# A two-layer decoder trunk on one core: 256-column score and value products in parts, an alternating token order behind attention groups, rotary tables in steps

## The chip, the cores and the metric

One core of one Trainium2 chip runs the kernel; the metric is the device time in microseconds. Matrix products run on TensorE, elementwise work on VectorE and ScalarE, weights come from memory by DMA queues that SyncE issues. In the views of the profile PE is TensorE, PEld its weight load, DVE is VectorE, ACT is ScalarE, POOL is GpSimd and SP is SyncE.

## The reference

Two layers on 256 tokens, a model width of 2048, 16 heads of 128. Each layer is: RMS norm, mixer, residual; RMS norm, gated feed-forward with a causal convolution of width 3, residual; an embedding projected and gated, residual.

```
layer 0 mixer: q,k,v = h @ w_in
   heads 0..7  : stick-breaking: z = q k^T * scale (strictly causal)
                 w = exp(log_sigmoid(z) + suffix sum of log_sigmoid(-z));  out = w @ v
   heads 8..15 : q,k partly rotated (first 32 of 128), three dilated windows
                 mixed by their log-sum-exp;  out = p @ v
layer 1 mixer: q,k,v and 16 forget gates from one projection
   s = q k^T * scale + c_q - c_k  (c: running sum of log gates), causal softmax;  out = p @ v
both: h += out @ w_out
feed-forward: u = conv3(norm(h) @ w_up);  h += (silu(gate) * value) @ w_down
embedding: h += sigmoid(norm(h) @ w_gate) * (p[i] @ w_ple)
```

## The kernel before

**Products in parts.** The activations lie with features on partitions and tokens along the free axis: `X` and `Y` are tiles of 128 partitions by 16 (or up to 16) feature blocks by 2 parts by 256 tokens. Each float32 number is held as two numbers of the type `F32R`, a high part (a copy that is rounded) and a low part (the difference). A product takes three matmuls, high by high, high by low and low by high: `PARTS = ((0, 0), (0, 1), (1, 0))`, line 206. Weights are read from DRAM in one stream in the order of use and split into parts on the chip: ScalarE casts (line 176), VectorE subtracts (line 177).

**The stream of weight products.** A unit is up to four blocks of 128 rows by 256 columns of a weight matrix. `gemm_unit` (line 208) makes up to 24 matmuls of 256 tokens from a unit, with the weight as the stationary operand; `gemm_v` (line 243) makes the values, with tokens as the stationary operand and 256 weight columns moving; `gemm_vf` (line 256) does so with 272 columns for the first values of layer 1 and the gates. `unit` (line 183) has three units split ahead, in a ring of four.

**Attention between units.** Each finished unit is a tick. `defer(n, fn)` (line 194) puts a function at the n-th tick from now, and `tick` (line 197) runs what is due. `head_pair` (line 579) makes q, k and v of two heads with four units each and defers the attention of the pair among the units that follow: `first` (scores and softmax or stick-breaking, 2 to 4 ticks after k), `second` (4 or 5 ticks later) and `attend` (2 ticks later). So a pair's scores stand behind its values, its second step inside the next pair's q or k, its values product inside the next pair's k. TensorE takes its work in this order; the other engines are ordered by a planner unless a place is marked to keep the program's order. `norm_finish` defers the norm's sums and rows; `with_rows` holds back what needs the rows.

**The attention's matmuls** before the change are in full float32, except the suffix sums of the stick-breaking heads (lines 459 to 467), which are in parts, and the row of the gates' sums (line 481):

- `sb_first`, line 438 (128 columns, keys of the second half) and line 441 (256 columns, keys of the first half by all queries).
- `sm_first`, line 483 (128 columns, first half of the queries) and line 485 (256 columns, second half of the queries by all keys).
- `sm_second`, line 520: six transposes of 128x128 of the softmax's weights, then one copy of 768 columns out of PSUM (line 522).
- `attend`, line 529 (128 columns) and line 532 (256 columns): values by weights.

A float32 matmul shows as two records in the trace, a matmul on parts as one. q and k lie in tiles `q` and `k`, the scaled values in `v` (written at lines 588 and 621 by ScalarE).

**The rotary tables** (`rope_tables`, line 401) are sines and cosines of 32 rows by 256 tokens, some twenty VectorE operations with two ScalarE sines, called after pair 1 of layer 0 and first read by `rope` for pair 4. The page's names for tiles: `psq`, `psk`, `psv`, `pso`, `psu`, `psd`, `psg`, `psp` are the products of the weight matrices (q, k, v, output, up, down, gate, embedding), `scs` the scores, `sps` the second step, `avp` the values product.

Of the kernel before, what the change touches and what calls it, by code (L numbers as in the profile page):

```python
# [104 lines left out]
def trunk(ctx: ExitStack, tc: tile.TileContext, xT, pT, pos, gains, conv, bf, cst, wst, out):  # L105
# [20 lines left out]
    rT = cpool.tile([P, 2], F32, name="rT")  # L126

    root = cpool.tile([P, 2], F32, name="root")
# [19 lines left out]
    at = {"group": 0, "off": 0, "unit": 0, "tick": 0, "rows": 0}  # L148
# [58 lines left out]

    def gemm_unit(ps, act, kind, l, c0, k0, first, last, koff=0):

        kc, w = unit(kind, l, k0, c0)  # L210
        order = [(j, k, n) for j in range(2) for k in range(kc) for n in range(3)]
        if at["tick"] == 0:

            order.sort(key=lambda o: o[2])
        for i, (j, k, n) in enumerate(order):
            s, t = PARTS[n]
            nc.tensor.matmul(ps[:, j, :], lhsT=w[:, k, s, j * P:(j + 1) * P], rhs=act[:, k0 - koff + k, t, :],  # L217
                             start=first and i == 0,
                             stop=last and k == kc - 1 and n == 2, skip_group_check=True)
        tick()  # L220
# [22 lines left out]
    def gemm_v(ps, act, l, c0):  # L243

        for i in range(4):
            kc, w = unit("w_in", l, 4 * i, c0)
            for t in range(2):
                tsl = slice(t * P, (t + 1) * P)
                for k in range(kc):
                    for n, (a, b) in enumerate(PARTS):  # L250
                        nc.tensor.matmul(ps[:, t], lhsT=act[:, 4 * i + k, a, tsl], rhs=w[:, k, b],  # L251
                                         start=i + t + k + n == 0,
                                         stop=i == 3 and k == kc - 1 and n == 2, skip_group_check=True)
            tick()
# [146 lines left out]
    def rope_tables():  # L401
        ang = t2_tile("ang", (32, S))
        n = t2_tile("angn", (32, S))
# [4 lines left out]
        for step in (4096.0, 1.0):  # L408
# [13 lines left out]
        nc.vector.scalar_tensor_tensor(out=n, in0=ang, scalar=-1.0, in1=ang,  # L422
                                       op0=ALU.mult, op1=ALU.min)
        nc.vector.tensor_scalar_add(out=n, in0=n, scalar1=math.pi / 2)
        nc.scalar.activation(out=rc, in_=n, func=AF.Sin)
# [9 lines left out]
    def sb_first(q, k):  # L435
# [4 lines left out]
        for j in range(2):  # L440
            nc.tensor.matmul(sc[:, 0, j * S:(j + 1) * S], lhsT=k[:, j, 0:128], rhs=q[:, j, :],
                             start=j == 0, stop=True, skip_group_check=True)
# [14 lines left out]
    def sb_second(z, e, eh, el):  # L457
# [3 lines left out]
        for i, x in enumerate((eh, el)):  # L461
# [6 lines left out]
                         start=False, stop=True, skip_group_check=True)  # L468
        nc.vector.tensor_sub(out=z, in0=z, in1=sp.rearrange("p a b -> p (a b)")[:, :768])
        nc.scalar.activation(out=e, in_=z, func=AF.Exp)  # L470
        return e
# [3 lines left out]
    def sm_first(q, k, fox):  # L475
        sc = at_tile("scs")
        for j in range(2):
            if fox is not None:
# [6 lines left out]
            nc.tensor.matmul(sc[:, j, 128:384], lhsT=q[:, j, 128:256], rhs=k[:, j, :],  # L485
                             start=False, stop=True, skip_group_check=True)
# [27 lines left out]
    def sm_second(pe, s):  # L514
# [10 lines left out]
    def attend(hp, w, v, dst):  # L525
        av = at_tile("avp")
        for j in range(2):
            js = slice(j * P, (j + 1) * P)
            nc.tensor.matmul(av[:, 0, j * S + 128:(j + 1) * S], lhsT=v[:, 1, js],  # L529
                             rhs=w[:, 512 + j * P:512 + (j + 1) * P], start=j == 0, stop=False,  # L530
                             skip_group_check=True)
            nc.tensor.matmul(av[:, 0, j * S:(j + 1) * S], lhsT=v[:, 0, js], rhs=w[:, j * S:(j + 1) * S],  # L532
                             start=False, stop=True, skip_group_check=True)
# [45 lines left out]
    def head_pair(l, hp, act, dst, st):  # L579
        q = work.tile([P, 2, S], F32, name="q", tag="qkv", bufs=2)  # L580
        k = work.tile([P, 2, S], F32, name="k", tag="qkv", bufs=2)
        v = work.tile([P, 2, S], F32, name="v", tag="v", bufs=1)
        full = _cuts(KT)
        if l % 2 == 1 and hp == 0:
            ps = at_tile("psv")
            gemm_vf(ps, act, l)
            for t in range(2):
                nc.scalar.activation(out=v[:, t, :], in_=ps[:, t, 0:S], func=AF.Copy,
                                     scale=rT[:, t:t + 1])
            st["fox"] = forget_gates(l, ps)  # L590
        ps = mm_tile("psq")
# [7 lines left out]
        def first():  # L599
            if l % 2 == 0 and hp < 4:  # L600
                a = sb_first(q, k)
                defer(5, lambda: second(lambda: sb_second(*a)))
            else:
                a = sm_first(q, k, st["fox"] + (2 * hp,) if l % 2 == 1 else None)
# [9 lines left out]

        defer(late + (2 + (l % 2 == 0 and hp >= 4) if hp == 7 or (l % 2 == 1 and hp == 0) else 4), first)
# [4 lines left out]
        for i in range(2):  # L620
            nc.scalar.activation(out=v[:, i, :], in_=ps[:, i, :], func=AF.Copy, scale=rT[:, i:i + 1])
# [29 lines left out]
    for l in range(DEPTH):  # L651
        st = {}
        if l == 0:
# [13 lines left out]
            norm_finish(True, 12, 14)  # L667
        for hp in range(NH // 2):
# [3 lines left out]
            if l % 2 == 0 and hp == 1:  # L672
                rope_tables()
# [158 lines left out]
```

## Time and profile before

| | |
|---|---|
| time, median of 3 runs | 2422.07 us (2421.6 to 2423.37) |
| profiled execution, time and span | 2423.39 us, 2421.6 us |
| mean granted TensorE clock | 0.998 |
| DMA | 458.05 MB, mean 189 GB/s |
| weight products of w_up (`psu`, line 217) | 8448 matmuls, 959.7 us |
| weight products of w_down (`psd`, line 217) | 4224 matmuls, 479.7 us |
| casts of weights (line 176), ScalarE | 874, 901.2 us |
| differences of weights (line 177), VectorE | 874, 1045.8 us |

The profile is of one execution. Its page gives busy times of each engine, the chain of work that ended last (followed back from the last instruction), and groups of instructions with count, busy time and mean duration. Matmuls are pipelined: a record's duration (some 276 ns) overlaps the next one's, so the time that a matmul costs is read from the distance of the starts, or from the chain's pieces, whose length is the time that they hold the chain.

### The profile page before, as it was taken

The page shows a single profiled execution, that of the slowest core. Times are in us where ns is not written, and L with a number is a line of the kernel's source. Part 1 is how long each engine was busy: PE and PEld are TensorE (multiplying, and loading weights), DVE is VectorE, ACT ScalarE, POOL GpSimd, SP SyncE. Part 2 cuts the span into 40 slices and gives each one's busy share as a digit, 9 for nine tenths or more (in the row PEclk, how much of TensorE's full clock was granted, in tenths as well). Part 3 has the DMA queues.
Part 4 walks back from the last instruction along what each step waited for, and adds up shares of the span by engine and source line. Part 5 has one row for each costly group of instructions (what it writes and reads, how often), then busy time and mean ns, then how long its engine had stood idle before and what let it go on. Part 6 is the DMA issues. An engine that isn't in the chain of part 4 may idle for free.

```text
span 2421.6 us, 47927 instructions
## 1 busy us (share of the span) xinstructions
PE 2406.9 (99%) x20992; PEld 2400.8 (99%) x20992; DVE 1581.7 (65%) x2066; ACT 1228.6 (51%) x1546; POOL 5.9 (0%) x13
## 2 busy tenths in 40 slices
PE   9999999999999999999999999999999999999998
PEld 9999999999999999999999999999999999999997
DVE  7666766776567657767755555667665776567666
ACT  6554455554355445555554444555544554455554
POOL 0000000000000000000000000000000000000000
PEclk9999999999999999999999999999999999999999
DMA  7454445555555555555554454555555555555553
GB/s 284 167 181 171 174 182 192 192 193 193 196 197 197 186 199 192 193 186 203 183 188 174 167 181 163 198 190 195 192 192 193 194 195 191 202 193 187 186 203 122
DMA packets 66818, 458.05 MB, mean 189 GB/s; under 512 B 7552, under 2 KB 7840, under 8 KB 16944
## 3 DMA queue, kind: packets, MB, share of 16 engines
q1 hardware_dynamic: 66576, 454.93, 53.0%
q8 instruction: 164, 2.69, 0.4%
q14 instruction: 46, 0.38, 0.0%
q0 software_dynamic: 32, 0.06, 0.0%
HBM read 452.86 MB, written 2.10 MB: 188 GB/s over the span
## 4 chain that ended last, share of the span: by engine, by line
PE 98%; DMA 1%; DVE 0%; SPq 0%; ACT 0%; issue 0%; POOLq 0%; DVEq 0%; ACTq 0%
PE psu L217 40%; PE psd L217 20%; PE psk L217 7%; PE pso L217 7%; PE psq L217 7%; PE psv L251 7%; PE psg L217 7%; DMA wr<-in_w 1%; PE avp L532 1%; PE psv L264 1%; PE psp L217 0%; PE pse L730 0%; PE scs L485 0%; PE sps L520 0%; PE avp L529 0%; PE scs L483 0%
## 5 line engine op out<-in xcount | busy, mean ns | idle before, releaser
L177 DVE TENSOR_TENSOR w<-wr,w 128x1024 fp32r<-128x1024 f32 (+2 forms) x874 | 1045.8, 1198 | 686.0 <-ACT w L176 681.4
L176 ACT CAST w<-wr 128x1024 fp32r<-128x1024 f32 (+2 forms) x874 | 901.2, 1031 | 1063.1 <-PE psu L217 354.3
L217 PE MATMUL psu<-act,w 128*128 128x256 f32 x8448 | 959.7, 276 | 0.0
L217 PEld LDWEIGHTS psu<-act,w 128*128 128x128 f32 x8448 | 958.4, 188 | 0.1
L217 PE MATMUL psd<-act,w 128*128 128x256 f32 x4224 | 479.7, 276 | 0.0
L217 PEld LDWEIGHTS psd<-act,w 128*128 128x128 f32 x4224 | 479.2, 188 | 0.0
L217 PE MATMUL psk<-act,w 128*128 128x256 f32 x1536 | 184.8, 279 | 0.0
L217 PE MATMUL psq<-act,w 128*128 128x256 f32 x1536 | 183.1, 279 | 1.1 <-DVE act L285 0.9
L217 PEld LDWEIGHTS psk<-act,w 128*128 128x128 f32 x1536 | 180.0, 188 | 0.8
L217 PEld LDWEIGHTS psq<-act,w 128*128 128x128 f32 x1536 | 178.7, 188 | 2.1 <-DVE act L285 1.1
L217 PE MATMUL pso<-act,w 128*128 128x256 f32 x1536 | 176.5, 277 | 0.0
L217 PEld LDWEIGHTS pso<-act,w 128*128 128x128 f32 x1536 | 175.6, 188 | 0.1
L251 PE MATMUL psv<-w,act 128*128 128x256 f32 x1440 | 167.4, 277 | 0.0
L251 PEld LDWEIGHTS psv<-w,act 128*128 128x128 f32 x1440 | 165.6, 188 | 0.1
L217 PE MATMUL psg<-act,w 128*128 128x256 f32 x1440 | 164.8, 276 | 0.0
L217 PEld LDWEIGHTS psg<-act,w 128*128 128x128 f32 x1440 | 163.9, 188 | 0.1
L630 DVE TENSOR_TENSOR u<-psu,rb 128x512 f32<-128x512 f32 x88 | 60.9, 692 | 33.0 <-PE psu L217 32.8
L636 DVE SCALAR_TENSOR_TENSOR yv<-u,cv,yv 128x256 f32<-128x256 f32 x176 | 73.4, 480 | 0.0
L636 DVE SCALAR_TENSOR_TENSOR yg<-u,cv,yg 128x256 f32<-128x256 f32 x176 | 73.3, 479 | 0.0
L633 ACT ACTIVATE yg<-u,cv 128x256 f32<-128x256 f32 x88 | 48.0, 593 | 1.1 <-DVE u L630 1.1
L633 ACT ACTIVATE yv<-u,cv 128x256 f32<-128x256 f32 x88 | 47.9, 592 | 0.0
L275 ACT CAST act<-yg 128x512 fp32r<-128x512 f32 x44 | 27.4, 622 | 39.2 <-DVE yg L646 39.2
(165 smaller groups left out, 880.7 us busy)
## 6 DMA issues: line engine op xcount, KB each, us to landing
wr<-in_w SPq DMA_DIRECT2D x388, 1024.0 KB, 4.8
wr<-in_w SPq DMA_DIRECT2D x36, 768.0 KB, 4.3
wr<-in_w SPq DMA_DIRECT2D x8, 896.0 KB, 4.6
h<-in_x SPq DMA_DIRECT2D x4, 512.0 KB, 9.0
wr<-in_w SPq DMA_DIRECT2D x4, 512.0 KB, 10.5
out_dram<-h SPq DMA_DIRECT2D x7, 256.0 KB, 2.4
wr<-in_w SPq DMA_DIRECT2D x2, 816.0 KB, 4.3
pl<-in_w SPq DMA_DIRECT2D x3, 512.0 KB, 7.9
```

What stands on the lines that cost most here:

```text
L176: nc.scalar.copy(out=w[:, :, 0, :], in_=raw)
L177: nc.vector.tensor_sub(out=w[:, :, 1, :], in0=raw, in1=w[:, :, 0, :].bitcast(F32))
L217: nc.tensor.matmul(ps[:, j, :], lhsT=w[:, k, s, j * P:(j + 1) * P], rhs=act[:, k0 - koff + k, t, :], start=first and i == 0, stop=last and ...
L251: nc.tensor.matmul(ps[:, t], lhsT=act[:, 4 * i + k, a, tsl], rhs=w[:, k, b], start=i + t + k + n == 0, stop=i == 3 and k == kc - 1 and n = ...
L264: nc.tensor.matmul(ps[:, t, :n], lhsT=act[:, k0 + k, a, t * P:(t + 1) * P], rhs=w[:, k, b, :], start=k0 + k + i == 0, stop=k0 + k == KT - ...
L275: nc.scalar.copy(out=dst[:, :, 0, :], in_=src)
L532: nc.tensor.matmul(av[:, 0, j * S:(j + 1) * S], lhsT=v[:, 0, js], rhs=w[:, j * S:(j + 1) * S], start=False, stop=True, skip_group_check=True)
L630: nc.vector.tensor_mul(out=u[:, :, 2:], in0=ps, in1=rb2)
L633: nc.scalar.activation(out=y[:, j, :], in_=u[:, j, 2:], func=AF.Identity, bias=cv[:, l, t, 3:4], scale=cv[:, l, t, 2:3])
L636: nc.vector.scalar_tensor_tensor(out=y[:, j, :], in0=u[:, j, tap:tap + S], scalar=cv[:, l, t, tap:tap + 1], in1=y[:, j, :], op0=ALU.mult, ...
```

## The change

Three things are changed.

1. Products with 256 columns in the scores and values are made in parts. `in_parts` and `tile_parts` split one of q and k into parts in full and one 128-token half of the other; `in_parts` splits the 256-column share of the attention weights; `values` makes parts of the first half of the values. Lines 441, 485 and 532 become three matmuls each. The products with 128 columns stay in float32.
2. `shake` sets a count of 2. The next two matmuls that `gemm_unit` or `gemm_v` issue then take their moving columns, and write their output, in another order: 8 from the first half, 8 from the second, and so on (`walk`). Each column still lands in its place. `shake` is called behind each group of scores, of suffix sums or transposes and of values products, behind the forget gates, and at two ticks of the start.
3. The rotary tables are made in five steps, two ticks apart, with the tables' own tiles as scratch. Two small tiles, `rT` and `root`, become one.

```diff
+    def walk(ap):
+        return ap.rearrange("p (a b c) -> p b a c", a=2, c=8)
+    def shake():
+        at["shake"] = 2
+    def walks(*aps):
+        if not at["shake"]:
+            return aps
+        at["shake"] -= 1
+        return [walk(x) for x in aps]
...
-            nc.tensor.matmul(ps[:, j, :], lhsT=w[:, k, s, j * P:(j + 1) * P], rhs=act[:, k0 - koff + k, t, :],
+            to, rows = walks(ps[:, j, :], act[:, k0 - koff + k, t, :])
+            nc.tensor.matmul(to, lhsT=w[:, k, s, j * P:(j + 1) * P], rhs=rows,
...
-        ang = t2_tile("ang", (32, S))
-        n = t2_tile("angn", (32, S))
+        ang, n = rc, rs
...
+                if bits in (11, None):
+                    yield
...
+    def in_parts(x, name):
+        hi, lo = t2_tile(name + "h", dt=F32R), t2_tile(name + "l", dt=F32R)
+        nc.scalar.copy(out=hi, in_=x)
+        nc.vector.tensor_sub(out=lo, in0=x, in1=hi.bitcast(F32))
+        return hi, lo
+    def tile_parts(x):
+        xp = t2_tile("xp", (P, 2, 2, P), F32R)
+        nc.scalar.copy(out=xp[:, 0], in_=x)
+        nc.vector.tensor_sub(out=xp[:, 1], in0=x, in1=xp[:, 0].bitcast(F32))
+        return xp[:, 0], xp[:, 1]
...
         for j in range(2):
-            nc.tensor.matmul(sc[:, 0, j * S:(j + 1) * S], lhsT=k[:, j, 0:128], rhs=q[:, j, :],
-                             start=j == 0, stop=True, skip_group_check=True)
+            for n, (a, b) in enumerate(PARTS):
+                nc.tensor.matmul(sc[:, 0, j * S:(j + 1) * S], lhsT=one[a][:, j, :], rhs=full[b][:, j, :],
+                                 start=j + n == 0, stop=n == 2, skip_group_check=True)
+        shake()
...
         nc.scalar.activation(out=e, in_=z, func=AF.Exp)
-        return e
+        return in_parts(e[:, 0:512].rearrange("p (j s) -> p j s", j=2), "w"), e[:, 512:768]
...
-            nc.tensor.matmul(sc[:, j, 128:384], lhsT=q[:, j, 128:256], rhs=k[:, j, :],
-                             start=False, stop=True, skip_group_check=True)
+            for n, (a, b) in enumerate(PARTS):
+                nc.tensor.matmul(sc[:, j, 128:384], lhsT=one[a][:, j, :], rhs=full[b][:, j, :],
+                                 start=False, stop=n == 2, skip_group_check=True)
+        shake()
...
-        w = s.rearrange("p a b -> p (a b)")
-        nc.scalar.copy(out=w, in_=sp.rearrange("p a b -> p (a b)")[:, :768])
-        return w
+        shake()
+        w = in_parts(sp[:, 0, :].rearrange("p (j s) -> p j s", j=2), "w")
+        w1 = s.rearrange("p a b -> p (a b)")[:, 0:256]
+        nc.scalar.copy(out=w1, in_=sp[:, 1, 0:256])
+        return w, w1
+    def values(v, t, ps):
+        if t == 0:
+            nc.scalar.activation(out=v[0][:, 0, :], in_=ps, func=AF.Copy, scale=rT[:, 0:1])
+            nc.vector.scalar_tensor_tensor(out=v[0][:, 1, :], in0=ps, scalar=rT[:, 0:1],
+                                           in1=v[0][:, 0, :].bitcast(F32), op0=ALU.mult, op1=ALU.subtract)
+        else:
+            nc.scalar.activation(out=v[1], in_=ps, func=AF.Copy, scale=rT[:, 1:2])
...
-            nc.tensor.matmul(av[:, 0, j * S:(j + 1) * S], lhsT=v[:, 0, js], rhs=w[:, j * S:(j + 1) * S],
-                             start=False, stop=True, skip_group_check=True)
+            for n, (a, b) in enumerate(PARTS):
+                nc.tensor.matmul(av[:, 0, j * S:(j + 1) * S], lhsT=v[0][:, a, js], rhs=w[b][:, j, :],
+                                 start=False, stop=n == 2, skip_group_check=True)
+        shake()
...
+        def prepare():
+            if l % 2 == 0 and hp < 4:
+                st["parts"] = in_parts(q, "f"), tile_parts(k[:, :, 0:128])
+            else:
+                st["parts"] = in_parts(k, "f"), tile_parts(q[:, :, 128:256])
+        with_rows(prepare)
...
+            for n in (5, 8):
+                defer(n, shake)
...
             if l % 2 == 0 and hp == 1:
-                rope_tables()
+                steps = rope_tables()
+                for i in range(5):
+                    defer(2 + 2 * i, lambda: next(steps, None))
```

More of the change, by code (lines that the diff above doesn't have):

```diff
@@ L125, in trunk @@
     rq = cpool.tile([P, S], F32, name="rq")
-    rT = cpool.tile([P, 2], F32, name="rT")
-    root = cpool.tile([P, 2], F32, name="root")
+    rr = cpool.tile([P, 4], F32, name="rr")
+    rT, root = rr[:, 0:2], rr[:, 2:4]
     nc.gpsimd.memset(root, -0.5)
@@ L147, in trunk @@
     raws, ready = [], []
-    at = {"group": 0, "off": 0, "unit": 0, "tick": 0, "rows": 0}
+    at = {"group": 0, "off": 0, "unit": 0, "tick": 0, "rows": 0, "shake": 0}
     def issue_group():
@@ L250, in gemm_v @@
                     for n, (a, b) in enumerate(PARTS):
-                        nc.tensor.matmul(ps[:, t], lhsT=act[:, 4 * i + k, a, tsl], rhs=w[:, k, b],
+                        to, cols = walks(ps[:, t], w[:, k, b])
+                        nc.tensor.matmul(to, lhsT=act[:, 4 * i + k, a, tsl], rhs=cols,
                                          start=i + t + k + n == 0,
@@ L432, in rope, with sb_first @@
         nc.vector.tensor_add(out=x[:32], in0=x[:32], in1=sw)
-    def sb_first(q, k):
+    def in_parts(x, name):
[8 more added lines that the diff above has]
+        return xp[:, 0], xp[:, 1]
+    def sb_first(q, k, prepared):
+        full, one = prepared
         sc = at_tile("scs")
@@ L468, in sb_second, with sm_first @@
                          start=False, stop=True, skip_group_check=True)
+        shake()
         nc.vector.tensor_sub(out=z, in0=z, in1=sp.rearrange("p a b -> p (a b)")[:, :768])
         nc.scalar.activation(out=e, in_=z, func=AF.Exp)
-        return e
+        return in_parts(e[:, 0:512].rearrange("p (j s) -> p j s", j=2), "w"), e[:, 512:768]
     SEG = ((0, 128), (128, 384))
-    def sm_first(q, k, fox):
+    def sm_first(q, k, prepared, fox):
+        full, one = prepared
         sc = at_tile("scs")
@@ L528, in attend @@
             js = slice(j * P, (j + 1) * P)
[L529 to L532, printed above, removed]
-                             start=False, stop=True, skip_group_check=True)
+            nc.tensor.matmul(av[:, 0, j * S + 128:(j + 1) * S], lhsT=v[1][:, js], rhs=w1[:, j * P:(j + 1) * P],
+                             start=j == 0, stop=False, skip_group_check=True)
+            for n, (a, b) in enumerate(PARTS):
+                nc.tensor.matmul(av[:, 0, j * S:(j + 1) * S], lhsT=v[0][:, a, js], rhs=w[b][:, j, :],
+                                 start=False, stop=n == 2, skip_group_check=True)
+        shake()
         parts(dst[:, 2 * hp:2 * hp + 2], av[:, 0, :].rearrange("p (j s) -> p j s", j=2))
@@ L581, in head_pair @@
         k = work.tile([P, 2, S], F32, name="k", tag="qkv", bufs=2)
-        v = work.tile([P, 2, S], F32, name="v", tag="v", bufs=1)
+        v = (work.tile([P, 2, S], F32R, name="vp", tag="vp"), work.tile([P, S], F32, name="v", tag="v"))
         full = _cuts(KT)
@@ L587, in head_pair @@
             for t in range(2):
-                nc.scalar.activation(out=v[:, t, :], in_=ps[:, t, 0:S], func=AF.Copy,
-                                     scale=rT[:, t:t + 1])
+                values(v, t, ps[:, t, 0:S])
             st["fox"] = forget_gates(l, ps)
+            shake()
         ps = mm_tile("psq")
@@ L600, in first @@
             if l % 2 == 0 and hp < 4:
-                a = sb_first(q, k)
+                a = sb_first(q, k, st["parts"])
                 defer(5, lambda: second(lambda: sb_second(*a)))
             else:
-                a = sm_first(q, k, st["fox"] + (2 * hp,) if l % 2 == 1 else None)
+                a = sm_first(q, k, st["parts"], st["fox"] + (2 * hp,) if l % 2 == 1 else None)
                 defer(4, lambda: second(lambda: sm_second(*a)))
@@ L620, in head_pair @@
         for i in range(2):
-            nc.scalar.activation(out=v[:, i, :], in_=ps[:, i, :], func=AF.Copy, scale=rT[:, i:i + 1])
+            values(v, i, ps[:, i, :])
     def ffn_group(l, g, g0, act, hid):
```

7 lines of the change are left out of this document (4 added, 3 removed).

## The prediction

> **What bounds the kernel now.** I read the head of the page first: the busy times, and the chain of work that ended last.
>
> ```profile
> span 2421.6 us, 47927 instructions
> ## 1 busy us (share of the span) xinstructions
> PE 2406.9 (99%) x20992; PEld 2400.8 (99%) x20992; DVE 1581.7 (65%) x2066; ACT 1228.6 (51%) x1546; POOL 5.9 (0%) x13
> ...
> PE 98%; DMA 1%; DVE 0%; SPq 0%; ACT 0%; issue 0%; POOLq 0%; DVEq 0%; ACTq 0%
> ```
>
> The reader is to see that TensorE and its weight loads are each busy 99% of the span, and that the chain is TensorE for 98% of it. So an edit counts by what it does to the sum of TensorE's pitches (start of one matmul to start of the next); work on VectorE (65%) and ScalarE (51%) counts only where TensorE has to wait for it. The second view is the chain in order of time (start, length, what). There a piece's length divided by its count is the pitch.
>
> ```profile
> 30.80 11.31 PE psk L217 x96
> ...
> 211.67 0.66 PE sps L520 x6
> 212.32 5.66 PE psk L217 x48
> ...
> 219.29 5.46 PE psk L217 x48
> ...
> 661.01 152.32 PE psu L217 x1344
> ...
> 1218.90 8.48 PE psq L217 x72
> ...
> 1514.52 5.66 PE pso L217 x48
> ```
>
> The weight products are all of one form (256 columns, weights and data in parts), and yet they run at **two pitches**. 152.32/1344 = 113.3 ns is the fast one, the same over the whole feed-forward part. 11.31/96 = 117.8 ns is the slow one, as are 8.48/72 and, with the step out of the transposes in it, 5.66/48. The difference is 4.5 ns for each product. The pitch holds for a stretch and turns only at something irregular: slow behind the six 128-column transposes (L520) at 212.32, fast again behind the values (L532, just ahead of 219.29; 5.46/48 with the first steps in it). From the matmuls' starts I count 11 of the 12 transposed groups with 48 slow products behind them (first 212.32, last 1514.52: 528), and outside them 215 at the start (the 96 at 30.80 among them), 72 at 1218.90, and behind some scores 96, 96, 84 and 48: 1,139 in all, so 5.1 us of the span.
>
> **The change part by part.**
>
> *Scores and values in parts.*
>
> ```profile
> 70.64 0.44 PE scs L438 x4
> 71.09 0.87 PE scs L441 x4
> ```
>
> ```profile
> L485 PE MATMUL scs<-k,q 128*128 128x256 f32 x48 | 14.3, 380 | 0.0
> L532 PE MATMUL avp<-s,v 128*128 128x256 f32 x48 | 14.3, 380 | 0.0
> ```
>
> A full-precision product of 256 columns is two records at 0.87/4 = 217 ns, so 0.434 us. The grouped rows give 48 records each to the scores and the values of the 12 softmax pairs, which is four a pair; the 4 stick-breaking pairs have as many a pair. That is 16 pairs x 8 / 2 = 64 products. Each becomes three products in parts, of the form of the weight products. At the fast pitch that is 0.340 us, at the slow one 0.353 us. The saving is 64 x 0.094 = 6.0 us or 64 x 0.081 = 5.2 us. I take 5.2, because the three now stand behind 128-column work (L529, L483: 0.44/4 = 110 ns a record, like the transposes), and behind that the slow pitch is what these rows show. The 128-column products stay as they are. In the values and the dilated scores the step from full precision to parts now comes once more in each group. By the records' starts the last transpose (28 ns) and the first product behind it (201 ns) together take 229 ns against 109 + 118 = 227 for the two at their own pitches, so some 20 such steps cost under 0.2 us.
>
> *Tokens alternately from two halves.* There are 8 calls behind scores, 8 behind the weights and 8 behind the values in each layer, two at the start and one behind the forget gates: 51, hence 102 products with their moving columns and their output read in pieces of 8. What this pattern costs no row shows. From below: nothing, and a gain on the products themselves is excluded, since they move the same 256 columns behind the same weight load. The nearest row with an output in pieces is L464, whose 256 columns go into two separate runs of 128:
>
> ```profile
> 85.81 0.12 PE sps L462
> 85.92 0.12 PE sps L464
> ```
>
> It takes 0.12 us, as L462 with its one run does. From above I take a half-rate product, the 217 ns of a full-precision record: 104 ns more, 102 x 0.104 = 10.6 us. The pieces are 16 times more than in L464, so I do not take nothing; I take 15 ns a product, near that row: **1.5 us**. The Trainium skill, in "SBUF — State Buffer" (the box on cachelines under Door 1), speaks against the change here: it says that any non-contiguous PSUM access pattern significantly slows matmuls. L464 does not bear that out for long runs, and no run here shows it for runs of 8; by that rule the sum stands nearer to the upper end, which is a rival below.
>
> What the pattern does to the products *behind* it is the larger question. A state that holds over hundreds of products and turns at an irregular one should turn at two products of another length or order. If it turns to fast each time, it takes away the slow stretches listed above, all but about 50 products at the start that run ahead of the first call: 1,089 x 4.5 ns = **4.9 us**.
>
> *What is added on VectorE and ScalarE.* Per head pair: two splits of 128x512 (one of q or k, one of the weights), one of 128x256, and one more VectorE operation for the values.
>
> ```profile
> L176 ACT CAST w<-wr 128x512 fp32r<-128x512 f32 x8 | 5.0, 622 | 13.3 <-PE psv L251 11.6 <-PE psk L217 1.7
> ```
>
> ```profile
> L285 DVE SCALAR_TENSOR_TENSOR act<-h,gn,act 128x256 fp32r<-128x256 f32 x96 | 41.9, 478 | 0.1
> ...
> L177 DVE TENSOR_TENSOR w<-wr,w 128x512 fp32r<-128x512 f32 x8 | 5.5, 692 | 8.5 <-ACT w L176 8.5
> ```
>
> ```profile
> 70.00:326.00 256.00, 256.00 (x2180) 254.02 (x2179) 166.06 (x205) 131.69 (x168) 0.00 (x0) 1.00 0.49 174
> ```
>
> VectorE gets 0.69 + 0.69 + about 0.45 + 0.48 = 2.3 us a pair, 18 us on its 166 in the layer's 256 us (the windows row: TensorE, weight load, VectorE, ScalarE): 65% becomes 72%. ScalarE gets about 1.3 us a pair, less behind the transposes, where one copy is cut to three. Neither becomes the bound. What counts is whether parts are late for TensorE, behind which all its products would then queue. The tightest place is a stick-breaking group's weights:
>
> ```profile
> 108.98 0.85 ACT L470 ACTIVATE e<-z 128x768 f32<-128x768 f32 x1
> 109.74 1.04 ACT L176 CAST w<-wr 128x1024 fp32r<-128x1024 f32 x1
> ```
>
> ```profile
> 112.29 0.43 PE avp L532 x2
> ```
>
> The weights are ready at 109.83 and the first 256-column product wants them at about 112.2. A copy of 0.62 and a difference of 0.69 end at 111.2, 1 us early; if the cast in between (1.04) goes first, about 112.2, just in time. Price without the cover: at most 0.7 us in each of 4 groups. The second is the first pair of the second layer, whose scores come 4.5 us after its k:
>
> ```profile
> 1242.33 1.36 PE psp L217 x12
> ...
> 1246.81 0.43 PE scs L485 x2
> ```
>
> k (0.69), two casts and two differences (0.62 + 0.69 + about 0.8) and one weight difference in the way (1.23) make 4.0 us of the 4.5. If late, under 1 us, once. The delayed weight casts are made for the product unit after next, and a unit takes 2.7 us, so a delay of 0.6 us does not reach TensorE. I cost all of this at nothing, with 0 to 4 us as bounds.
>
> *The rotary tables in steps.* Some twenty operations of 0.3 to 0.4 us leave VectorE's queue around 57 to 70 us and come in five steps, two units apart, ahead of the dilated heads that read them. They are not in the chain now and have some 60 us until q of the fifth pair, so nothing changes on TensorE; they only make room for the first pairs' new splits. On ScalarE the sine may need one more table load between exponentials; it is off the chain too. The merged small tiles cost nothing.
>
> **The sum.** - 5.2 + 0.2 + 1.5 - 4.9 = - 8.4 us. The profiled execution took 2423.39 us around its span of 2421.6, 0.05% over the median of 2422.07; the difference carries to the median: **2413.7 us**.
>
> **The rivals.**
>
> *The slow pitch stays (slower than before).* Until now scores and values ended in full-precision records of 217 ns, and behind these the pitch mostly came back to fast (219.29 above). They will end in products in parts. If the two alternating products do not turn the state, all weight products from the first scores to the norm's sums at the start of the feed-forward part are slow.
>
> ```profile
> 71.95 5.46 PE psk L217 x48
> ...
> 407.47 5.57 PE psu L217 x48
> ...
> 1608.90 5.57 PE psu L217 x48
> ```
>
> From 71.95 to 407 and from 1248 to 1608 there are, less some 56 us of attention groups and at 113 to 114 ns, about 5,630 of them, some 850 slow already: 4,780 x 4.5 ns = 21.5 us lost, 5.2 - 0.2 gained: 2438.6 us. It decides against the change from about 1,100 more slow products on. For it: 11 of 12 groups that end in 128-column work leave the slow pitch. Against it: the state turned to fast behind each values group of these eleven.
>
> *The alternating order is dear.* At half rate 102 products lose 10.6 us; with the rest as forecast: 2422.8 us, no change. This is where the skill's rule above leads.
>
> *The order does nothing.* Stretches stay as slow or fast as now, and only the products in parts are left: 2422.07 - 5.0 = 2417.1 us, at the edge of what can be told. The skill's "TensorE: Matmul & The Clock Gate" (Part 2, step 1) gives TensorE two independent read ports, one for moving data and one for weights, so that one would not slow the other; by that, the order of the tokens would not matter to the products behind. The two pitches in the rows above show that something outside that rule acts.
>
> *Late parts.* The new splits come late at scores or values, 0.1 to 0.3 us in each of 32 places: 3 to 8 us back, 2417 to 2422 us. Against it are the two covers worked out above.
>
> **How the numbers follow.** Forecast 0.60; slow pitch stays 0.14; dear order 0.12; order does nothing 0.08; late parts 0.06. About 0.2% (4.8 us, limit 2417.2) is what a measurement of this kernel can tell from no change. Faster takes the forecast and about half of "does nothing" and little of the rest: 0.65. Same takes the dear order and what is left: 0.20. Slower: 0.15. The low end is both gains in full (6.0 + 4.9) with free alternating products and a little over: 2410. The high end takes in the dear order and the late parts, 2424, and leaves out the slow pitch.
>
> **What would show it.** Scores and values rows with 128x256 products in parts, three for each of 64, at 113 to 118 ns. Weight products behind transposes at 113.3 (48 in 5.44 us instead of 5.66), likewise at the start from 34 us on. The alternating pairs at no more than 130 ns. TensorE's idle time in the waits unchanged. I am wrong if the stretches behind scores and values show 117.8, if the alternating pair takes 200 ns, or if TensorE waits for parts.

## The result and the profile after

The changed kernel takes **2437.07 us** (median of 6 runs, 2434.39 to 2438.67). The kernel before, run beside it, takes 2422.57 us (2421.32 to 2423.52). The ratio is 1.0059, with a 95% interval of 1.0046 to 1.0072. The change costs 14.5 us where the prediction had a gain of 8.4 us. The prediction was wrong in its sign, and the result lies outside its range.

The profiled execution of the changed kernel took 2434.39 us around a span of 2432.2 us. That is the shortest of its six, 2.7 us under the median. The two profiles therefore explain 10.6 us of span; the other 3.9 us between the medians are in no trace. The mean granted clock gives a hint: it was 0.998 in the three shortest of the six executions (2434.39 to 2436.7 us) and 0.996 or 0.997 in the three longest (2437.44 to 2438.67). The last section shows what this may be; for the changed kernel itself it is not shown.

First two groups of the kernel before (count, then busy us and mean ns of one), then the head of the page of the changed kernel and the same two groups:

```profile
L217 PE MATMUL pso<-act,w 128*128 128x256 f32 x1536 | 176.5, 277 | 0.0
L251 PE MATMUL psv<-w,act 128*128 128x256 f32 x1440 | 167.4, 277 | 0.0
```

```profile
span 2432.2 us, 48172 instructions
## 1 busy us (share of the span) xinstructions
PE 2416.6 (99%) x21056; PEld 2414.8 (99%) x21056; DVE 1613.5 (66%) x2130; ACT 1246.2 (51%) x1594; POOL 5.9 (0%) x13
...
L232 PE MATMUL pso<-act,w 128*128 128x256 f32 x1536 | 181.3, 281 | 0.0
...
L267 PE MATMUL psv<-w,act 128*128 128x256 f32 x1440 | 172.3, 279 | 0.0
```

TensorE is still busy 99% of the span, and VectorE has gone from 65% to only 66%. TensorE has 64 records more (64 products of two records became 64 of three). The two groups are weight products, as many as before, of the same shape and on the same weights; only the few that stand right behind an attention group take their tokens in the other order. The output's 1536 were 176.5 us before and are 181.3 us now; the values' 1440 went from 167.4 to 172.3 us. So the time went into products that are *all but unchanged*, and it did so with no new idle time before them (the 0.0 at the end).

Where it went is seen in the chain of work in order of time (start, length, what). A stretch of values products, and the second half of the output projection of the first layer, before the change:

```profile
224.75 10.88 PE psv L251 x96
...
325.07 0.43 PE avp L532 x2
325.51 73.46 PE pso L217 x648
```

And after it, the same places, with the group of transposes (line 559) and what follows it (this answers to the rows from 211.67 to 219.29 in the prediction):

```profile
213.94 0.66 PE sps L559 x6
214.59 5.48 PE psk L232 x48
...
220.88 0.35 PE avp L583 x3
221.23 5.66 PE psk L232 x48
226.90 11.31 PE psv L267 x96
...
328.29 0.35 PE avp L583 x3
328.64 76.33 PE pso L232 x648
...
667.33 152.32 PE psu L232 x1344
```

Three things are to be seen. The values product itself is shorter, as the prediction had it: 0.35 us for three products in parts where 0.43 us stood for one in full precision. The 48 products behind the transposes (L559) have turned to the fast pitch, also as forecast: 5.48 instead of 5.66 us. But the weight products behind a values group, up to the next group, have turned to the slow pitch, behind all 16 of them: 5.66 us for 48 instead of 5.46, 11.31 for 96 instead of 10.88, and 76.33/648 = 117.8 ns instead of 73.46/648 = 113.4 ns. The two pitches have changed places, and the stretches behind values are much the longer ones. The feed-forward part is as it was, 152.32 us for 1344.

The whole account, from the starts of all matmuls in the two traces: each attention group is taken from its first record to the third product behind it, less two products at 113.3 ns; the remaining products are split into what exceeds 113.3 ns by up to 25 ns (the pitch) and by more (waits).

| us | before | after | difference | forecast |
|---|---|---|---|---|
| 16 score groups | 23.94 | 21.59 | -2.35 | |
| 16 values groups | 21.21 | 18.72 | -2.49 | scores and values: -5.2 + 0.2 |
| 16 second steps (suffix sums, transposes) | 11.70 | 11.97 | +0.27 | all alternating products, in this row and the two above: +1.5 |
| products over 113.3 ns by the pitch | 6.46 | 21.16 | **+14.70** | -4.9 |
| products held up by more (waits) | 3.25 | 3.93 | +0.68 | 0 |
| the small groups (norms, gates, start) | 16.36 | 16.40 | +0.04 | 0 |
| sum | | | +10.9 | -8.4 |

The sum is the 10.6 us of span but for 0.3. Counted, some 1,130 products ran at the slow pitch before and some 4,470 do after.

### The profile page after: what moved, and what is told of

It reads as the page before. It is cut to its first block, busy times and chain, and to the rows that moved or that the text cites. A ratio compares the mean times of both kernels' runs of the same rounds, so it can differ in the third digit from the quotient of the medians.

```text
span 2432.2 us, 48172 instructions
## 1 busy us (share of the span) xinstructions
PE 2416.6 (99%) x21056; PEld 2414.8 (99%) x21056; DVE 1613.5 (66%) x2130; ACT 1246.2 (51%) x1594; POOL 5.9 (0%) x13
## 4 chain that ended last, share of the span: by engine, by line
PE 98%; DMA 1%; DVE 1%; SPq 0%; issue 0%; ACT 0%; POOLq 0%; DVEq 0%
PE psu L232 39%; PE psd L232 20%; PE pso L232 7%; PE psk L232 7%; PE psv L267 7%; PE psq L232 7%; PE psg L232 7%; PE psv L280 0%; PE avp L583 0%; PE psp L232 0%; PE pse L795 0%; DMA h<-in_x 0%; PE scs L523 0%; DMA cv<-in_conv 0%; PE sps L559 0%; PE avp L580 0%
## 5 line engine op out<-in xcount | busy, mean ns | idle before, releaser
L232 PEld LDWEIGHTS psk<-act,w 128*128 128x128 f32 x1536 | 181.3, 189 | 0.1
L232 PE MATMUL pso<-act,w 128*128 128x256 f32 x1536 | 181.3, 281 | 0.0
L232 PEld LDWEIGHTS pso<-act,w 128*128 128x128 f32 x1536 | 180.6, 189 | 0.0
L267 PE MATMUL psv<-w,act 128*128 128x256 f32 x1440 | 172.3, 279 | 0.0
L267 PEld LDWEIGHTS psv<-w,act 128*128 128x128 f32 x1440 | 170.7, 188 | 0.0
```

Source lines behind the costliest of these rows:

```text
L232: nc.tensor.matmul(to, lhsT=w[:, k, s, j * P:(j + 1) * P], rhs=rows, start=first and i == 0, stop=last and k == kc - 1 and n == 2, skip_gr ...
L267: nc.tensor.matmul(to, lhsT=act[:, 4 * i + k, a, tsl], rhs=cols, start=i + t + k + n == 0, stop=i == 3 and k == kc - 1 and n == 2, skip_gr ...
```

## The experiments

Two theories were set against each other for the slow stretches. **Theory A**: what *ends* a group decides. A full-precision record of 217 ns leaves TensorE at the fast pitch and a product in parts leaves it at the slow one; the alternating pair does nothing. **Theory B**: the alternating pair itself turns it to slow. Four kernels separate the two.

### The changed kernel without the alternating order

```diff
     def shake():
-        at["shake"] = 2
+        at["shake"] = 0
```

> The changed kernel with the alternating token order taken out; products in parts and the rotary steps stay. Theory A (the end of a group decides: a 217 ns full-precision record just ahead of the weight products brings the fast pitch back, products in parts behind 128-column records leave it slow; the alternating pair only turns the stretches behind the transposes and some scores): these stretches turn slow too, some 20 of 48 to 96 products by 4.5 ns, so 3 to 6 us more than the changed kernel, about 2441 us. Theory B (the alternating pair itself throws the products into the slow pitch): the stretches turn fast again, and with the 5 us of the products in parts the time is about 2417 us.

Measured: 2437.1 us, ratio 1.0059 [1.0044, 1.0074], the same as the changed kernel. The long stretch, in the chain:

```profile
329.68 76.32 PE pso L232 x648
```

117.8 ns without a single alternating product. The slow pitch comes without the alternating order (behind all 16 values groups, some 4,620 slow products), so theory B does not hold as the only cause. What this kernel has over the kernel before are the products in parts, with their splits and tiles, and the tables in steps; the tables are out, since the kernel with these alone (below) keeps all 16 stretches behind values fast. Theory A's own number, some 4 us above this, was missed too: the stretches behind the 12 groups of transposes are all fast here, with nothing alternating.

### The kernel before, with the alternating order alone

```diff
+    def shake():
+        at["shake"] = 2
...
+            to, rows = walks(ps[:, j, :], act[:, k0 - koff + k, t, :])
...
+        shake()
```

at the same 51 places; scores and values stay in full precision, the tables as before.

> The kernel before with only the alternating pairs added at the same places; scores and values stay in full precision. Theory A: behind values and scores the pitch stays fast as before, behind the transposes the pair turns it to fast (11 stretches of 48 by 4.5 ns = 2.4 us, and part of the start), so 2418 to 2420 us. Theory B: the stretches behind scores and values turn slow as in the changed kernel, some 3300 products by 4.5 ns = 15 us, about 2437 us.

Measured: 2436.68 us, ratio 1.0057 [1.0042, 1.0072].

```profile
328.37 0.43 PE avp L550 x2
328.80 76.33 PE pso L230 x648
```

The group ends in the 217 ns records (0.43 us for two) and the stretch behind is slow nevertheless, as are 15 of the 16 behind values. That is theory B's number, and theory A as the only cause falls. Behind the transposes the same pairs do the opposite: all 12 stretches are fast, where 11 were slow before. The two parts of the change *each* turn the long stretches to slow, and together they do no more than either. The distances from start to start behind the values groups, worked out from the traces, one typical row each in ns (the last record of the group, then the products):

```
before             28 | 310 118 117 115 115 113 113 114 113 113 114 113
alternating_only   28 | 307 122 119 118 119 117 118 118 117 118 118 118
no_alternating    119 | 114 118 118 117 118 118 118 117 118 118 118 117
after             118 | 120 121 119 119 118 118 117 118 118 117 119 117
```

In the first row the pitch has come down to 113 by the sixth product. In the second, two alternating products stand at the head, and it stays at 118. An alternating product itself is not dear: 119 to 122 ns.

### Six alternating products instead of two

If two products of another order can turn the state at all, their number may matter.

```diff
     def shake():
-        at["shake"] = 2
+        at["shake"] = 6
```

> The changed kernel with six alternating products behind each group instead of two. If each alternating product adds a little lag and the state turns once enough has gathered, the slow stretches behind scores and values turn fast: 15 us less, and 204 more alternating products at 4 to 8 ns cost 1 to 2 us, so about 2423 us or less. If their number does not matter, 2437 to 2440 us, with 117.8 ns behind the values as now.

Measured: 2423.69 us, ratio 1.0005 [0.9995, 1.0015].

```profile
327.12 73.52 PE pso L232 x648
```

The long stretch is fast again, and 13.4 us come back against the changed kernel. Behind the values the pitches now read:

```
alternating_six   118 | 119 122 121 125 122 125 118 115 123 118 114 113
```

All 16 stretches behind values are fast. But 10 of the 12 stretches behind transposes are slow (206 125 122 127 120 121 119 120 117 118 behind the first of them), where two had left 10 of them fast.

### Parts in one head of two, full precision last

```diff
-        for j in range(2):
-            for n, (a, b) in enumerate(PARTS):
...
+        for n, (a, b) in enumerate(PARTS):
+            nc.tensor.matmul(sc[:, 0, 0:S], lhsT=one[a][:, 0, :], rhs=full[b][:, 0, :],
+                             start=n == 0, stop=n == 2, skip_group_check=True)
+        nc.tensor.matmul(sc[:, 0, S:2 * S], lhsT=k[:, 1, 0:128], rhs=q[:, 1, :],
+                         start=False, stop=True, skip_group_check=True)
```

and likewise in the softmax scores and in the values, with no alternating products.

> No alternating order; of each pair only the first head's 256-column scores and values are in parts, the second head's stay in full precision and stand last in the group. Theory A: each group of scores and values ends in 217 ns records again, so the stretches are as in the kernel before (about 1100 slow products), and half the saving is left, 32 x 0.081 = 2.6 us: about 2420 us. Theory B says nothing else here; but if it is the products in parts anywhere in the group, or the shifted tiles, that bring the slow pitch, it stays at 2435 us or more.

Measured: 2423.11 us, ratio 1.0002 [0.9993, 1.0012].

```profile
324.65 0.43 PE avp L595 x2
325.08 73.45 PE pso L232 x648
```

Against the kernel without the alternating order, this one changes what stands last in a group; it also halves the products in parts and shapes their tiles anew, and these were not tried apart. All 16 stretches behind values are fast, as theory A has it where nothing alternates. Behind scores theory A fails: there too the group ends in full precision, and yet all 8 stretches behind the second layer's scores are slow, where 2 of them were in the kernel before. Its time was expected lower by some 3 us. Half of the groups' gain is there (scores 22.92 us, values 19.89 us: 2.3 us less than before), but a wait at the start gives most of it back. That led to the third part of the change.

### The rotary tables in steps alone

In the waits of TensorE one row has grown. Before the change, and after it:

```profile
PE psq L217 <- DVE act L285: 0.9, 1, 0.9
```

```profile
PE psq L232 <- DVE act L301: 2.8, 1, 2.8
```

The prediction did not look there, since the tables were to leave a place more than 30 us later. The experiment is the kernel before with this edit alone:

```diff
-        ang = t2_tile("ang", (32, S))
-        n = t2_tile("angn", (32, S))
+        ang, n = rc, rs
...
+                if bits in (11, None):
+                    yield
...
-                rope_tables()
+                steps = rope_tables()
+                for i in range(5):
+                    defer(2 + 2 * i, lambda: next(steps, None))
```

> The kernel before with only the rotary tables in steps and the tables' own tiles as scratch. Theory C: without scratch tiles of the ring the planner starts the tables at some 24 us, ahead of the last parts of x on VectorE, and TensorE waits 2 to 3 us for these at its 73rd q product (2.8 us in the run with six alternating products, 0.9 us before): 1.5 to 3 us more than before, about 2425 us. Rival: the wait at the start is only the landing of x, which differs from run to run: no difference, 2422.8 us.

Measured: 2425.53 us, ratio 1.0011 [1.0002, 1.0020], so +2.6 us. VectorE's timeline of that kernel (start, length, engine, line, operation) shows how:

```profile
24.29 0.27 DVE L403 CAST rc<-posi 32x256 f32<-32x256 int32 x1
...
25.61 2.20 DVE L416 SCALAR_TENSOR_TENSOR rc<-rs,rc 32x256 f32<-32x256 f32 x5
...
28.05 1.21 DVE L177 TENSOR_TENSOR w<-wr,w 128x1024 fp32r<-128x1024 f32 x1
29.18 1.26 DVE L285 SCALAR_TENSOR_TENSOR act<-h,gn,act 128x256 fp32r<-128x256 f32 x3
```

From 24.29 to 28.1 us VectorE works at the first steps of the tables, *ahead* of the last weights' difference and the last parts of x (L285), for which TensorE's first unit of q waits. The edit defers the steps by ticks, but it also makes the tables' own tiles the scratch. The scratch before came from a ring of buffers and had to wait for its turn; `rc` and `rs` are free from the beginning, and the planner moves the operations into a gap more than 30 us ahead of the old place. In the kernel before, the same timeline has the gap, with the next difference waiting 1.57 us for its cast:

```profile
26.02 1.23 DVE L177 TENSOR_TENSOR w<-wr,w 128x1024 fp32r<-128x1024 f32 x1 [1.57 <-ACT w L176]
```

The first steps of the tables take 3.8 us (24.29 to 28.05), so they overrun it by 2. All 16 stretches behind values are fast in this kernel and 11 of the 12 behind transposes slow, as before, so the tables alone do not turn the pitch. That the scratch is what lets them move, and not the deferral, is argued from the edit; the two were not tried apart. That the early place makes the wait is shown by the last two experiments, which move it: TensorE's wait there is 0.9 and 0.6 us in them.

### Six alternating products, the tables as before

```diff
-        at["shake"] = 2
+        at["shake"] = 6
...
-        ang, n = rc, rs
+        ang = t2_tile("ang", (32, S))
+        n = t2_tile("angn", (32, S))
...
-                steps = rope_tables()
-                for i in range(5):
-                    defer(2 + 2 * i, lambda: next(steps, None))
+                rope_tables()
```

> Products in parts, six alternating products, but the rotary tables as before the change. Theory C: the run with six alternating products less 1.5 to 3 us, so 2420.5 to 2422 us, a little under the kernel before. Rival (the start differs from run to run only): 2423.7 us as with the steps.

Measured: 2423.97 us, ratio 1.0003 [0.9994, 1.0012]; no gain over the version with steps. The first wait is back at 0.9 us, and two others have come, in TensorE's waits:

```profile
PE avp L582 <- ACT wh L456: 1.0, 1, 1.0
PE psq L232 <- DVE act L301: 0.9, 1, 0.9
PE avp L579 <- ACT e L505: 0.7, 1, 0.7
```

ScalarE's timeline says what is late:

```profile
106.01 1.28 ACT L438 ACT_TABLE_LOAD   x1
108.17 0.51 ACT L438 ACTIVATE rs<-ang,ct 32x256 f32<-32x256 f32 x1 [0.88 <-DVE ang L437]
108.93 0.42 ACT L442 ACTIVATE rc<-angn 32x256 f32<-32x256 f32 x1 [0.25 <-DVE angn L441]
109.84 1.28 ACT L505 ACT_TABLE_LOAD   x1 [0.49 <-DVE z L504]
111.13 0.84 ACT L505 ACTIVATE e<-z 128x768 f32<-128x768 f32 x1
111.88 1.03 ACT L176 CAST w<-wr 128x1024 fp32r<-128x1024 f32 x1
```

The sines come ahead of the second pair's exponential, which then ends at 111.97, with a weight cast and the new split of the attention weights still behind it. This is the late-parts rival, and its tight place is the one that the prediction named (a stick-breaking group's weights); but it needs the tables at once *and* the new splits. In the changed kernel the steps had kept it away.

### Where the tables and the numbers are chosen apart

Two versions with the tables at once: six behind scores, suffix sums and values and two behind the transposes (`def shake(n=6)`, with `shake(2)` in `sm_second`), and four everywhere (`at["shake"] = 4`).

> As six_tables_at_once, but two alternating products behind the weights' step (transposes, suffix sums) and six behind scores and values. In the changed kernel two turned the pitch to fast behind 9 of 12 transposed groups, all where the pitch ahead of them was fast; with six behind them it stays slow. If the state is a matter of how much lag has gathered at each place, 9 or more stretches of 48 by 4.5 ns = 2 us come off: 2418.5 to 2420 us, 0.1 to 0.2% under the kernel before. If the turning cannot be carried over from one kernel to another, no better than six_tables_at_once.

> As six_tables_at_once with four alternating products. If a certain number has to be reached for the state to turn, behind the values either all 16 stretches are fast (2420 to 2422 us, as with six) or all are slow (2433 to 2436 us, as with two); a mixture would mean that the place decides more than the number.

Measured: 2421.22 us, ratio 0.9992 [0.9984, 1.0001], and 2421.18 us, ratio 0.9994 [0.9985, 1.0003]. Four behind values do what six do: all 16 stretches are fast with four, and with six all but the one just behind the late exponential. Two behind the transposes make all 12 of those fast, four do too, and six had left 10 of them slow. (The expectation for the first counts 9 of 12 fast in the changed kernel, all behind fast stretches. The trace has 10, and the one at 213.94 stands behind a slow stretch.) The late exponential costs both of them: from the scores of the second pair to those of the third they take 2.4 and 3.5 us longer than the kernel before. So the first, which was expected below 2420 us, missed by a microsecond, and neither can be told from the kernel before.

The last two hold the tables to the program's order, in steps, so that neither the early start nor the late exponential can come about:

```diff
-    def shake():
-        at["shake"] = 2
+    def shake(n=4):
+        at["shake"] = n
...
+        keep = tc.keep_in_program_order
-        nc.vector.tensor_copy(out=ang, in_=posi)
+        keep(nc.vector.tensor_copy(out=ang, in_=posi))
...
-        shake()
+        shake(2)
```

with `keep` around every operation of the tables, and two behind the suffix sums and the transposes. The second has six for four.

> Products in parts; four alternating products behind scores and values, two behind the weights' step; the rotary tables in steps, but held to the program's order so that they start behind the second pair's scores. Theory (three separate effects: the state behind each group, the tables at 24 us, the sine ahead of an exponential with the tables at once): no wait of 2.8 us at the start, no wait of 1.7 us at the second pair's values, stretches fast behind scores, values and transposes: the run with four and the tables at once less 3 us, 2418 to 2419 us, about 0.2% under the kernel before. If the tables only move their wait to another place, 2421 us.

> The same with six alternating products behind scores and values. By the same theory 64 more alternating products at 8 ns, 0.5 us above the run with four: 2418.5 to 2419.5 us. If four fails at some place where six does not, six is the faster by 2 us or more.

Measured: **2417.24 us**, ratio 0.9977 [0.9968, 0.9986], and 2418.07 us, ratio 0.9981 [0.9972, 0.9990]. The first is faster than both kernels of the case, by 5.8 us than the one before, run beside it. The two came out 0.8 and 0.4 us under the ranges expected of them. The rows of the first, of the waits and then of the chain:

```profile
PE psq L232 <- DVE act L301: 0.9, 1, 0.9
```

```profile
322.21 73.50 PE pso L232 x648
```

By the account above, its scores and values groups are 4.6 us shorter than before, its second steps 0.3 longer, its waits 1.1 and its pitch 1.5 us shorter: the change's first part pays what it was forecast to, once nothing else is lost. The 4.9 us that were to come from the slow stretches come to 1.5, because some 670 products stay slow and because the alternating products themselves cost a few ns each.

## Why the prediction was wrong

**What bounds the kernel: right.** TensorE's pitches are the whole account; VectorE and ScalarE did not become the bound.

**Products in parts, -5.2 us and +0.2 for the steps: right.** The scores and values groups became 2.35 + 2.49 = 4.8 us shorter, the alternating pairs behind them included; in the kernel without these pairs the same account gives 5.0 us.

**The alternating products, +1.5 us: too dear, without weight.** The second steps, whose own products stayed as they were, took 0.27 us more for 16 groups, and the pairs read 118 to 127 ns. The rival of the dear order (200 ns each) is out.

**The slow stretches, -4.9 us: this step failed.** It was put so: "A state that holds over hundreds of products and turns at an irregular one should turn at two products of another length or order. If it turns to fast each time, it takes away the slow stretches listed above". The first half holds, but that the pitch also turns at some changes from one kind of weight product to another (in the changed kernel twice from slow to fast, where psv ends and pso or psp begins). The second was an assumption about the *direction*, for which the traces of before had no row: no product of another order stood in them. The turn goes either way. In the kernel with the alternating order alone, two such products turned the stretches behind transposes from slow to fast (eleven slow of twelve before, none with them) and 15 of the 16 behind values from fast to slow. Besides, the sum gave the products in parts no effect on what stands behind them, and they turn the same stretches to slow without any alternating pair. In the changed kernel the term came out at +14.7 us. Its stretches behind transposes came out fast as forecast, but they are fast without the pairs too, as the first experiment shows.

**The rival that came true.** "The slow pitch stays" gave 2438.6 us; 2437.07 were measured. Its mechanism held for the products in parts: without any alternating order the stretches behind values are slow, and with full precision last they are fast. That its number came so near is luck: it counted 4,780 more slow products (21.5 us), where some 3,340 came (14.7 us), since the stretches behind transposes and most of those behind scores are fast; and 3.9 us of the measured difference are in neither trace. The prediction laid against it that "the state turned to fast behind each values group of these eleven". That was evidence about groups that ended in full precision, and the change took just that away. A chance of 0.14 was too little for it. It was also not the whole cause, since the alternating pair alone does the same to groups that still end in full precision.

**VectorE and ScalarE at nothing: right, but for a reason that was not given.** No wait for an attention part is in the changed kernel's trace. (The bound for late parts has a slip: 32 places at 0.3 us are 9.6 us, not 8. Nothing rests on it.) The cover of the second pair held because the tables were out of the way; with the tables at once TensorE waits there for 1.0 and 0.7 us.

**The rotary tables at nothing: the second step that failed, a smaller one.** They were said to leave VectorE's queue around 57 to 70 us and to change nothing on TensorE. Alone they cost 2.6 us; in the changed kernel's trace the first wait grew by 1.9 us, of which +0.68 is left in the account, as small waits for weights at the start went away. The missed part is that nothing held the steps to the place where they are written: the planner had a free gap and the edit's scratch had nothing to wait for.

**What stays open.** Which property of a group decides the state behind it was not found. For the stretches behind values the runs give a table that holds in nearly all of the 16 places: full precision last and nothing alternating, fast; parts last and nothing alternating, slow; two alternating behind either, slow; four or six behind parts, fast. Behind transposes: none in the kernel before, slow in 11 of 12; none in the two experiments without the alternating order, fast (in the kernel with parts in one head the stretch ahead of them is fast in the first layer and slow in the second, so a mere toggle is no answer); two, fast in 10 of 12 in the changed kernel and in all 12 in the four other kernels with two; four, fast; six, slow in 10. Behind scores no such table comes out: with full precision last and nothing alternating, 4 of 16 are slow in the kernel before and 8 of 16 in the one with parts in one head. The kernels with products in parts also have other tiles in memory, and whether their place matters was not tried. No single rule was found for these, and what in TensorE holds the state is not visible in the profile.

## What to carry to other kernels

Where one engine is busy 99% of the span, divide the lengths of the chain's pieces by their counts before *and* after an edit, for the instructions that were not edited: a few ns on thousands of them outweigh what the edit saves on 64. A state that a trace shows can be used in a forecast only in the directions that its rows show; for the other direction, give both signs a like chance and try the number of the irregular instructions on the chip, here two, four and six. When scratch is moved from a ring of buffers to tiles that are free from the start, look at the first place where the planner can now put the work, not only at the place where it is written.

## What was not expected of the hardware

The two pitches, 113.3 and 117.8 ns for one and the same form of product with the granted clock at 0.998 over the span (1.00 in the windows around the 648 products, before and after), hold until the next irregular instruction or change of product, for 648 products in the rows above. An attention group of about a microsecond and the few products behind it set which of them the whole stretch gets. Over the kernel that is a matter of 15 us, or 0.6%.

Runs of 8 in the moving columns and in the output are nearly free: the pairs take 118 to 127 ns where their neighbours take 113 to 118. The Trainium skill, in "SBUF — State Buffer" (the box on cachelines under Door 1), says that any non-contiguous PSUM access pattern significantly slows matmuls. For runs of 8 this trace does not agree.

A short wait of TensorE can cost more than its length. In the kernel with six alternating products and the tables at once, TensorE waited around 112 us for 1.7 us in all (windows: the stretch, its length, busy us of TensorE, weight load, VectorE, ScalarE and GpSimd, and then the granted clock):

```profile
110.00:112.00 2.00, 1.30 (x12) 1.10 (x10) 0.90 (x1) 1.99 (x3) 0.00 (x0) 1.00 0.57 238
112.00:114.00 2.00, 1.00 (x6) 0.82 (x7) 1.06 (x1) 2.00 (x3) 0.00 (x0) 1.00 0.00 0
114.00:116.00 2.00, 2.00 (x12) 2.00 (x12) 2.00 (x4) 0.91 (x2) 0.00 (x0) 0.58 0.26 57
116.00:118.00 2.00, 2.00 (x13) 2.00 (x12) 0.78 (x2) 0.59 (x1) 0.00 (x0) 0.57 0.95 401
```

Behind it the granted clock is 0.58 and 0.57 for 4 us. In the chain, the products from the end of the wait to the first values product (psv) behind it take 5.2 us (113.87 to 119.08). In the kernel with six and two the same wait stands at the same place, the clock stays at 1.00, and the same products take 3.7 us (114.07 to 117.76), so the clock costs another 1.5 us:

```profile
110.00:112.00 2.00, 1.50 (x14) 1.31 (x12) 1.10 (x1) 1.95 (x2) 0.00 (x0) 1.00 0.72 303
112.00:114.00 2.00, 0.80 (x4) 0.61 (x5) 0.85 (x1) 2.00 (x4) 0.00 (x0) 1.00 0.00 0
114.00:116.00 2.00, 2.00 (x19) 2.00 (x18) 2.00 (x3) 1.10 (x2) 0.00 (x0) 1.00 0.51 66
```

With four everywhere the clock falls at this place too (0.50 and 0.70). The wait at the start, 2.7 to 3.0 us in the five kernels that have the tables early, does the same in two of the five traces. In the kernel without the alternating order the rows behind it read:

```profile
30.00:32.00 2.00, 2.00 (x14) 2.00 (x14) 1.97 (x6) 2.00 (x4) 0.00 (x0) 0.74 0.67 238
32.00:34.00 2.00, 2.00 (x11) 2.00 (x11) 2.00 (x3) 0.07 (x1) 0.00 (x0) 0.50 0.71 295
```

Some 15 products stand about 213 ns apart there, and 17 in the kernel with six alternating products: 1.5 and 1.7 us. In the trace of the changed kernel the clock stays at 1.00 behind the same wait. Its longer executions have the lower mean clock, so some of them may hold such a stretch; that is not shown.

The Trainium skill, in "TensorE: Matmul & The Clock Gate" (Part 1), has a clock that falls to one half after an idle window of about 3.4 us, with windows that run freely and are not reset when the kernel starts. The fall to about one half and the free-running windows fit what is seen, where of like waits some are hit and some not; an idle time of 3.4 us is not needed by these rows, where TensorE was busy for 2.3 of the 4 us ahead, or had waited for 2.7 us. These are single profiles; of the other executions only the mean clock over the span is known, not where it fell.
